# VectorE takes GpSimd's low halves and products in projections, decays, solves and output projection of a hybrid decoder

## The chip, the cores and the metric

The kernel runs on one core of a Trainium2 chip, in one launch. The metric is the device time of one execution in microseconds; each row of the trace gives times from the start of that execution. The engines are named as in the profile: PE is TensorE's matmul and PEld its weight load, DVE is VectorE, ACT is ScalarE, POOL is GpSimd, SP is SyncE, which issues the DMAs.

## The reference

The kernel computes a decoder trunk of two layers on one sequence of 1024 tokens of width 1024, with 16 learned tokens in front. Cut to what matters here:

```python
h = concatenate([meta, x])                                    # 1040 tokens
for layer in range(2):
    proj = rmsnorm(h) @ w_in[layer]                           # 1024 x 3336
    y_a = hgrn2_mixer(...)     # silu(q), gates, scores of chunks with decays
    y_b = gdn_mixer(...)       # conv of 4 taps, silu, l2norm, decays, a triangular solve per chunk
    y_c = s5_mixer(...)        # a complex scan, gelu, a gate
    h = h + concatenate([y_a, y_b, y_c]) @ w_out[layer]       # 1024 x 1024
    h = h + relu(rmsnorm(h) @ w1[layer])**2 @ w2[layer]       # 1024 x 4096 x 1024
return rmsnorm(h)[:, 16:]
```

All inputs and outputs are float32.

## The kernel before

The 1040 tokens are worked in two halves of 520 (`T`), with features on the 128 partitions and tokens along the free axis, so a tile is mostly 128x520. Within a half, the recurrent mixers go by five windows of 104 tokens (`W`).

**Weights in two parts.** TensorE multiplies in the type fp32r. Each operand is therefore split in a high half (`wh`, `xh`, `uh`: a cast) and a low half (`wl`, `xl`, `ul`: the operand minus its high half), and each product takes three matmuls: high by high, high by low, low by high (`columns`, L499). Weights come in granules of 128x512 (`granule_now`, L467): SP loads `wr` from DRAM, ACT casts `wh`, and POOL subtracts to make `wl` (L475 through `split`, L457). `wr`, `wh` and `wl` have three buffers each, so SP can load a granule only when the subtraction has read the one three before it, and ACT can cast one only when PE has used the one three before it. One column of the input projection is 128 output features and takes two granules, 48 matmuls. A half of a layer has 26 such columns (52 granules) and one narrow one of eight features (`cols_ab`); the output projection has 16 granules, the MLP 128.

**Stages.** `run` (L1424) issues for each layer and each half: `block` (the input projection, the mixers) and `out_mlp` (the output projection, the MLP). Nothing is ordered by hand: the compiler's scheduler places each instruction on its engine's queue, with the order of issue as the priority, and the weights are moved ahead by 1000 places (`granule`, L462). Each engine then works its queue in that order. In the trace the projections and mixers of layer 0 lie in 45 to 650 us (both halves), those of layer 1 in 1100 to 1400 us and in 1850 to 2200 us, with MLP stretches between and behind them.

**Within a block.** `normed_rows` (L506) makes the eight `xh`, `xl` pairs and carries four columns of history from one half to the next (`hist`, L518 to L523, copied by POOL). `in_conv` (L645) makes a column, takes the four taps on DVE out of PSUM (`s<-pd,cvw,s`), then `silu` (L576): exp, ln, exp on ACT, and a product, which POOL makes. `in_silu`, `in_gate` and `in_hgrn` use the same `silu` for their columns; in all it is called 80 times. Between the columns, `gdn_decay` (L825) makes each window's decay matrices: `nh<-nh,gtok` on DVE, abs and exp on ACT, on POOL a product with the triangular masks (`mh<-nh,tri`, 104x416) and one with beta (`mh<-mh,gsc`, 104x208), then on DVE the product with the scores in PSUM (`mh<-mxt,mh`). That is ten windows and pairs of heads in each block, forty in all. `gdn_solve` (L871) inverts the diagonal blocks of 26 by 26: twelve small steps on DVE, then two products of blocks in pieces of 80x507, of which POOL makes every second one (L902), and its result goes to DRAM as `XD` (L909). `s5_layer` (L356, first half of a layer only) makes the state-space matrices with many small DVE products. `hgrn` (L1137) and `gdn_state` (L913) are the recurrences; they use POOL as well.

Of the kernel before, what the change touches and what calls it, by code (L numbers as in the profile page):

```python
# [9 lines left out]
F32 = mybir.dt.float32  # L10
# [3 lines left out]
ALU = mybir.AluOpType  # L14
# [7 lines left out]
T = 520  # L22
W = 104
# [21 lines left out]
HIST = 4  # L45
# [49 lines left out]
class Kern:  # L95
# [91 lines left out]
    def setup(self):  # L187

        nc = self.nc
        self.take(T)  # L190
        self.K, self.XD, self.SC, self.grp = {}, None, None, "h"
        warm = self.n([128, 2, 128])
        nc.vector.memset(warm, 0.0)
        for _ in range(7):
            self.mm(self.mps()[:, :256], warm[:, 0], warm.rearrange("p a b -> p (a b)"))
        self.ident = self.load_const("ident", [128, 128])
        nc.scalar.preload_act_table_set("natural_log_exp_and_others")
# [269 lines left out]
    def granule_now(self, fill, keep):  # L467
        raw = self.tl(self.big, [128, 4, 128], "wr", N_W)
        fill(raw)
        if keep:  # L470
            lo, hi = [self.operand(tag)[:, :512].rearrange("p (k m) -> p k m", k=4) for tag in ("xl", "xh")]
        else:
            lo = self.tl(self.big, [128, 4, 128], "wl", N_W, F32R)
            hi = self.tl(self.big, [128, 4, 128], "wh", N_W, F32R)
        self.split(raw, hi, lo, self.nc.gpsimd)  # L475
        return hi, lo

    def weights(self, ap):
# [24 lines left out]
    def normed_rows(self, h, wcol, b):  # L503

        nc = self.nc
        xs = [], []  # L506
        acc = self.s()
        for k in range(KD):
            self.square(acc, h[k], k)
        self.squares, self.r = acc, None  # L510
        r = self.scale()
        if b == 0:
            self.hist = self.tl(self.big, [128, KD, HIST], "hist", 1)
        for k in range(KD):
            w = self.prm[:, wcol + k:wcol + k + 1]
            xn = self.tl(self.sp, [128, T + 8], "s", N_S)[:, :T + HIST]
            if b == 0:
                nc.gpsimd.memset(xn[:, :HIST], 0.0)  # L518
            else:
                nc.gpsimd.tensor_copy(xn[:, :HIST], self.hist[:, k])  # L520
            self.stt(xn[:, HIST:], h[k], w, r, ALU.mult, ALU.mult)
            if b == 0:
                nc.gpsimd.tensor_copy(self.hist[:, k], xn[:, T:])  # L523
            hi, lo = self.operand("xh"), self.operand("xl")
            nc.scalar.copy(hi, xn)
            self.tt(lo, xn, hi.bitcast(F32), ALU.subtract)
            xs[0].append(hi)
            xs[1].append(lo)
        return xs
# [45 lines left out]

    def silu(self, n, out):  # L576
        self.sigma(out, n)
        self.tt(out, out, n, ALU.mult, eng=self.nc.gpsimd)

    def cols(self, l, col, xs, runs=None):  # L580
        wts = self.ready.pop((l, col), None) or self.in_weights(l, col)
# [5 lines left out]
    def cols_ab(self, l, xs):  # L587


        nc = self.nc  # L590
        wi = self.ins["w_in"][l].rearrange("(g k p) m -> g p k m", k=4, p=128)
        ps = self.tl(self.pd, [128, 2, 512], "pd", 2)
        for g in range(2):
            raw = self.tl(self.big, [128, 4, 128], "wr", N_W)[:, :, :8]
            w = self.tl(self.big, [128, 4, 128], "wh", N_W, F32R)
            nc.sync.dma_start(raw, wi[g][:, :, C_GA:C_GA + 8])
            nc.scalar.copy(w[:, :, 0:32].rearrange("p k (r m) -> p k r m", r=4), raw.unsqueeze(2).to_broadcast([128, 4, 4, 8]))
            self.tt(w[:, :, 32:40], raw, w[:, :, 0:8].bitcast(F32), ALU.subtract, eng=nc.gpsimd)
            for k in range(4 * g, 4 * g + 4):
                for c in range(2):  # L600
                    cs = slice(HIST + c * HN, HIST + (c + 1) * HN)
                    self.mm(ps[0:40, c, :HN], w[:, k % 4, 0:40], xs[0][k][:, cs], start=(k == 0), stop=False)
                    self.mm(ps[0:40, c, :HN], w[:, k % 4, 0:40], xs[1][k][:, cs], start=False, stop=(k == KD - 1))
        return ps
# [220 lines left out]
    def gdn_decay(self, g, w, pair):  # L825
        nc, K = self.nc, self.K
        it = NW * pair + w
        h0 = 2 * pair
        hs, ws = slice(h0, h0 + 2), slice(w * W, (w + 1) * W)
        qk = self.m()[:, :4 * W].rearrange("p (a b) -> p a b", a=4)  # L830
        self.load_heads(qk, g, 2, h0, ws)
        bc = self.decay_rows(g, w, h0, W)
        yield
        E = self.n([W, 2, W])
        self.tt(E, bc, self.gtok[:, w, 0, hs].unsqueeze(2).to_broadcast([W, 2, W]), ALU.subtract)
        yield
        ps = self.mps("t")
        pg = ps[:W, :4 * W].rearrange("p (a b c) -> p a b c", a=2, b=2)
        for h in range(2):
            self.mm(pg[:, 0, h, :], qk[:, 2 + h, :], qk[:, 2 + h, :])  # L840
            self.mm(pg[:, 1, h, :], qk[:, 2 + h, :], qk[:, h, :])
        self.act(E, E, AF.Abs)
        self.act(E, E, AF.Exp, scale=-1.0)
        yield
        ln, b2 = self.gln[:, w, hs], self.gsc[:, w, 3, hs]
        sq = self.n([W, 2, W])
        self.tt(sq, pg[:, 0], self.ident[:W, :W].unsqueeze(1).to_broadcast([W, 2, W]), ALU.mult)
        nc.vector.tensor_reduce(ln, sq, mybir.AxisListType.X, ALU.add)
        self.act(ln, ln, AF.Ln, bias=EPS)
        self.act(b2, ln, AF.Exp, scale=-1.0)  # L850
        MA = self.m()[:W, :4 * W].rearrange("p (a b c) -> p a b c", a=2, b=2)
        self.tt(MA, E.unsqueeze(1).to_broadcast([W, 2, 2, W]), K["tri"].unsqueeze(2).to_broadcast([W, 2, 2, W]), ALU.mult, eng=nc.gpsimd)
        self.tt(b2, b2, self.gsc[:, w, 1, hs], ALU.mult)
        yield
        self.tt(MA[:, 0], MA[:, 0], b2.unsqueeze(2).to_broadcast([W, 2, W]), ALU.mult, eng=nc.gpsimd)
        self.tt(MA, pg, MA, ALU.mult)
        yield
        nc.sync.dma_start(self.item(self.MAd, it), MA)
        if w == NW - 1:
            for h in range(2):  # L860
                p0 = NBK * NW * (2 * h + pair)
                nc.sync.dma_start(self.diag[p0:p0 + NW * NBK], self.blocks(self.MAd, NW * pair, NW, h * W))
        yield
# [10 lines left out]
    def gdn_solve(self):  # L874

        nc = self.nc
# [3 lines left out]
        H = SB // 2  # L880
# [14 lines left out]
        low = lambda t: t[:, H:, 0:H]  # L895
        mid = self.n([80, H, H])
        for dst, a, bt in ((mid, low(Dg), Tm[:, 0:H, 0:H]), (low(Tm), Tm[:, H:, H:], mid)):
            for n, i0 in enumerate(range(0, H, 3)):
                k = min(3, H - i0)
                prod = tmp()[:, :k * H * H].rearrange("p (i c j) -> p i c j", i=k, c=H)  # L900
                self.tt(prod, bt.rearrange("p j c -> p c j").unsqueeze(1).to_broadcast([80, k, H, H]),
                        a[:, i0:i0 + k, :].unsqueeze(2).to_broadcast([80, k, H, H]), ALU.mult, eng=nc.gpsimd if n % 2 else None)  # L902
                nc.vector.tensor_reduce(dst[:, i0:i0 + k, :], prod, mybir.AxisListType.X, ALU.add)
        Tt = Dg
        nc.scalar.copy(Tt, Tm.rearrange("p a b -> p b a"))
# [373 lines left out]
    def out_mlp(self, l, b, h, last=False):  # L1279
        nc = self.nc  # L1280
# [7 lines left out]
        for m in range(KD):  # L1288
            ps = self.product(self.weights(self.ins["w_out"][l][:, 128 * m:128 * m + 128]), xs)
            self.tt(self.half(h[m]), self.half(h[m]), ps, ALU.add)  # L1290
        xs = self.normed(h, 16 + 8 * l)
        NG = D_FF // 512
        hid = {}
# [134 lines left out]
    def run(self):  # L1428
        self.setup()
        self.H, self.YS = {}, {}  # L1430
        nxt = {}

        def early():

            nxt[1] = self.htiles()
            yield from self.load_x(1, nxt[1])
            self.save_h(1, nxt[1])
        h = self.htiles()
        trace(self.load_x(0, h))
        self.ready = {(0, col): self.in_weights(0, col) for col in (C_SU, C_SU + 128)}  # L1440
        self.setup_norms()
        self.block(0, 0, h, early(), True)
        self.block(0, 1, nxt[1])
        for l in range(DEPTH):
            for b in range(NB):

                self.take(512 if l + 1 == DEPTH and b == 0 else T)
                h = self.get_h(b)
                steps = self.out_mlp(l, b, h, l + 1 == DEPTH and b + 1 == NB)
                if l + 1 < DEPTH:  # L1450
                    self.save_h(b, h)
                    self.block(l + 1, b, h)
                else:
                    self.finish(b, h, steps)
# [29 lines left out]
```

## Time and profile before

| what | value |
|---|---|
| median of 3 runs | 3055.49 us (3043.4 to 3062.02) |
| the profiled execution, its own time | 3057.18 us |
| its span, first to last instruction | 3055.4 us |
| PE busy | 2826.1 us, 92% |
| DVE busy | 1562.6 us, 51% |
| POOL busy | 1580.1 us, 52% |
| ACT busy | 1298.7 us, 43% |
| mean granted clock of TensorE | 0.964 |

The shares are means over stages with different limits: in the MLP stretches PE is busy all the time and the other engines have little to do; in the projections and mixers every engine has work and PE is idle now and then. PE's busy time is no measure of how fast it works, since the granted clock and the width of the matmuls differ. A number like "mean ns" of an instruction counts from its start to its end, with any time in which it was held after its start.

### The profile page before, as it was taken

Reading aid. Unit: us, or ns where it says so; the run is one execution under the profiler, and the core shown is the slowest. Engines: PE = TensorE matmul, PEld = TensorE weight load, DVE = VectorE, ACT = ScalarE, POOL = GpSimd, SP = SyncE. Lnnn points to the kernel's source line nnn. Section 1 sums busy time; section 2 is a strip of 40 time slices with the busy share of each in tenths; the row PEclk is TensorE's granted clock in tenths of the full one; section 3 lists DMA queues with packets and bytes.
Section 4 is the critical chain, followed back from the end, with each engine's and each line's share of the span. In section 5 each row is a group of like instructions: output and inputs, shape, how many; then the busy total and the mean of one; then the engine's idle time right before and its main releaser. Section 6 shows DMA issues by size and latency. Waiting matters only on the chain.

```text
span 3055.4 us, 60525 instructions
## 1 busy us (share of the span) xinstructions
PE 2826.1 (92%) x23513; PEld 2637.9 (86%) x23513; DVE 1562.6 (51%) x2905; ACT 1298.7 (43%) x2657; POOL 1580.1 (52%) x1425
## 2 busy tenths in 40 slices
PE   7776899979999989878999998988999999999998
PEld 6775889978999989878999998986777788999998
DVE  7588664685532245787453224686554222522224
ACT  4434455534433345444444334543544333433332
POOL 4555465664644445747354444676464444444442
PEclk8898899989999999999999999999999999999999
DMA  5755555744433345555443334565443333533332
GB/s 148 193 125 160 141 154 138 213 95 125 126 96 96 91 141 142 161 142 149 130 115 96 94 91 142 144 152 152 113 125 98 100 96 95 163 91 90 93 91 80
DMA packets 641610, 381.17 MB, mean 125 GB/s; under 512 B 166239, under 2 KB 599237, under 8 KB 641325
## 3 DMA queue, kind: packets, MB, share of 16 engines
q1 hardware_dynamic: 641325, 377.31, 45.2%
q8 instruction: 186, 3.05, 0.4%
q14 instruction: 99, 0.81, 0.1%
HBM read 308.52 MB, written 70.43 MB: 124 GB/s over the span
## 4 chain that ended last, share of the span: by engine, by line
PE 45%; DVE 5%; issue 1%; DMA 1%; POOL 1%; ACT 1%; SPq 0%; DVEq 0%; POOLq 0%; ACTq 0%
PE pd L125 39%; PE mxt L125 4%; PE mxh L125 1%; DVE mh L113 1%; DVE s L116 1%; POOL wl L113 0%; DVE s L113 0%; ACT s L110 0%; DMA wr<-in_w_in_dram 0%; DVE s L121 0%; DMA nh<-rowd 0%; DVE mt L113 0%; POOL mh L113 0%; DVE ul L113 0%; DVE s L642 0%
## 5 line engine op out<-in xcount | busy, mean ns | idle before, releaser
L113 POOL TENSOR_TENSOR wl<-wr,wh 128x512 fp32r<-128x512 f32 x776 | 1025.2, 1323 | 1079.5 <-ACT wh L459 1012.3
L125 PE MATMUL pd<-xh,wh 128*128 128x260 f32 (+4 forms) x3688 | 832.3, 299 | 59.2 <-DVE s L116 21.2
L125 PE MATMUL pd<-xl,wh 128*128 128x260 f32 (+3 forms) x3688 | 830.1, 298 | 17.8 <-DVE xl L113 10.4
L459 ACT CAST wh<-wr 128x512 fp32r<-128x512 f32 x776 | 477.5, 617 | 862.5 <-PE pd L125 774.5
L125 PE MATMUL pd<-xh,wl 128*128 128x260 f32 (+2 forms) x3624 | 814.1, 299 | 11.0 <-POOL wl L113 10.7
L125 PEld LDWEIGHTS pd<-xh,wh 128*128 128x128 f32 (+1 forms) x3688 | 593.1, 192 | 81.4 <-issue 28.6
L125 PEld LDWEIGHTS pd<-xl,wh 128*128 128x128 f32 (+1 forms) x3688 | 594.4, 192 | 34.4 <-DVE xl L113 12.3
L125 PEld LDWEIGHTS pd<-xh,wl 128*128 128x128 f32 x3624 | 586.3, 193 | 27.2 <-POOL wl L113 13.5
L125 PE MATMUL pd<-uh,wh 128*128 128x260 f32 (+1 forms) x2008 | 469.5, 302 | 6.2 <-DVE h L113 3.6
L125 PE MATMUL pd<-ul,wh 128*128 128x260 f32 (+1 forms) x2008 | 470.5, 302 | 0.0
L125 PE MATMUL pd<-uh,wl 128*128 128x260 f32 (+1 forms) x2008 | 468.5, 302 | 1.2 <-POOL wl L113 1.2
L113 DVE TENSOR_TENSOR h<-h,pd 128x520 f32<-128x520 f32 (+2 forms) x296 | 200.4, 678 | 398.1 <-PE pd L125 395.5
L110 ACT ACTIVATE s<-s 128x520 f32<-128x520 f32 (+3 forms) x431 | 272.9, 635 | 196.5 <-DVE s L121 144.8
L125 PEld LDWEIGHTS pd<-uh,wh 128*128 128x128 f32 x2008 | 321.2, 189 | 22.3 <-issue 5.9
L125 PEld LDWEIGHTS pd<-uh,wl 128*128 128x128 f32 x2008 | 321.2, 189 | 15.4 <-POOL wl L113 2.1
L125 PEld LDWEIGHTS pd<-ul,wh 128*128 128x128 f32 x2008 | 321.4, 189 | 12.8
L116 DVE SCALAR_TENSOR_TENSOR s<-pd,r 128x520 f32<-128x520 f32 (+2 forms) x121 | 83.6, 692 | 330.8 <-PE pd L125 330.5
L113 DVE TENSOR_TENSOR ul<-s,uh 128x520 fp32r<-128x520 f32 (+1 forms) x129 | 97.7, 758 | 143.4 <-ACT uh L459 143.2
L113 POOL TENSOR_TENSOR s<-s 128x520 f32<-128x520 f32 x80 | 109.6, 1370 | 78.7 <-ACT s L110 67.9
L116 DVE SCALAR_TENSOR_TENSOR s<-pd,cvw,s 128x520 f32<-128x520 f32 x144 | 108.6, 754 | 46.4 <-ACT s L110 41.6
L113 POOL TENSOR_TENSOR mh<-mh,qh 128x260 f32<-128x260 f32 (+5 forms) x128 | 102.8, 827 | 29.9 <-ACT mh L110 29.3
L113 DVE TENSOR_TENSOR s<-s 128x520 f32<-128x520 f32 (+3 forms) x119 | 106.0, 895 | 21.8 <-ACT s L110 20.5
(255 smaller groups left out, 3187.9 us busy)
## 6 DMA issues: line engine op xcount, KB each, us to landing
wr<-in_mlp_w_dram SPq DMA_DIRECT2D x512, 256.0 KB
wr<-in_w_in_dram SPq DMA_DIRECT2D x208, 256.0 KB
wr<-in_w_out_dram SPq DMA_DIRECT2D x64, 256.0 KB
qkvd<-s SPq DMA_DIRECT2D x48, 260.0 KB
win<-qkvd SPq DMA_DIRECT2D x40, 312.0 KB
hdr<-h SPq DMA_DIRECT2D x32, 260.0 KB
mh<-qkvd SPq DMA_DIRECT2D x40, 208.0 KB
hd<-s SPq DMA_DIRECT2D x32, 260.0 KB
```

The costliest lines, as they stand in the source:

```text
L110: return self.nc.scalar.activation(out, in_, func, **kw)
L113: return (eng or self.nc.vector).tensor_tensor(out, a, b, op)
L116: return self.nc.vector.scalar_tensor_tensor(out, a, s, b, op0, op1)
L125: return self.nc.tensor.matmul(out, lhsT, rhs, start=start, stop=stop, **kw)
L459: self.nc.scalar.copy(hi, src)
```

## The change

Eight kinds of work leave POOL; POOL keeps the low halves of the MLP's weights and the products of `hgrn`, `gdn_state` and `s5`.

```diff
@@ setup
+        self.low = None
@@ granule_now
-        self.split(raw, hi, lo, self.nc.gpsimd)
+        self.split(raw, hi, lo, self.low)
@@ normed_rows
-                nc.gpsimd.tensor_copy(xn[:, :HIST], self.hist[:, k])
+                nc.scalar.copy(xn[:, :HIST], self.hist[:, k])
...
-                nc.gpsimd.tensor_copy(self.hist[:, k], xn[:, T:])
+                nc.scalar.copy(self.hist[:, k], xn[:, T:])
@@ silu
-        self.tt(out, out, n, ALU.mult, eng=self.nc.gpsimd)
+        self.tt(out, out, n, ALU.mult)
@@ cols_ab
-            self.tt(w[:, :, 32:40], raw, w[:, :, 0:8].bitcast(F32), ALU.subtract, eng=nc.gpsimd)
+            self.tt(w[:, :, 32:40], raw, w[:, :, 0:8].bitcast(F32), ALU.subtract)
@@ gdn_decay
-        self.tt(MA, E.unsqueeze(1)..., K["tri"].unsqueeze(2)..., ALU.mult, eng=nc.gpsimd)
+        self.tt(MA, E.unsqueeze(1)..., K["tri"].unsqueeze(2)..., ALU.mult)
...
-        self.tt(MA[:, 0], MA[:, 0], b2.unsqueeze(2)..., ALU.mult, eng=nc.gpsimd)
+        self.tt(MA[:, 0], MA[:, 0], b2.unsqueeze(2)..., ALU.mult)
@@ gdn_solve
-                        a[:, i0:i0 + k, :].unsqueeze(2)..., ALU.mult, eng=nc.gpsimd if n % 2 else None)
+                        a[:, i0:i0 + k, :].unsqueeze(2)..., ALU.mult)
@@ out_mlp, behind the output projection
+        self.low = nc.gpsimd
@@ run, behind out_mlp
+                self.low = None
```

By count, 272 subtractions `wl` of 128x512, 8 of `xl<-wr,xh` (the last eight granules, which are issued behind the last `out_mlp`), 80 silu products of 128x520, 40 products of 104x416, 40 of 104x208, 16 of 80x507 and 8 small ones of `cols_ab` go from POOL to DVE; 32 copies of 128x4 go from POOL to ACT. POOL keeps 504 `wl`. The scheduler, given other engines, also places other instructions anew. Lines behind L191 stand one further down in the changed kernel.

On DVE, in layer 1's first half, between the columns of the convolution where the decays begin (`s<-pd,cvw,s` are the taps, `nh`, `gln` the decays), there stood before:

```order
L121 TENSOR_SCALAR s<-s 128x520
L116 SCALAR_TENSOR_TENSOR s<-pd,cvw,s 128x520 x3
L121 TENSOR_SCALAR s<-s 128x520
L113 TENSOR_TENSOR nh<-mxt,ident 104x208
L113 TENSOR_TENSOR nh<-nh,gtok 104x208
L848 TENSOR_REDUCE gln<-nh 104x2
L113 TENSOR_TENSOR nh<-mxt,ident 104x208
L848 TENSOR_REDUCE gln<-nh 104x2
L113 TENSOR_TENSOR nh<-nh,gtok 104x208
```

The same place now:

```order
L113 TENSOR_TENSOR wl<-wr,wh 128x512
L113 TENSOR_TENSOR mh<-nh,tri 104x416
L116 SCALAR_TENSOR_TENSOR s<-pd,cvw,s 128x520 x2
L113 TENSOR_TENSOR s<-s 128x520
L116 SCALAR_TENSOR_TENSOR s<-pd,cvw,s 128x520
L113 TENSOR_TENSOR wl<-wr,wh 128x512
L121 TENSOR_SCALAR s<-s 128x520
L113 TENSOR_TENSOR nh<-mxt,ident 104x208
L113 TENSOR_TENSOR nh<-nh,gtok 104x208
L849 TENSOR_REDUCE gln<-nh 104x2
L113 TENSOR_TENSOR nh<-mxt,ident 104x208
L113 TENSOR_TENSOR wl<-wr,wh 128x512
```

Two subtractions and one silu product stand in each column's row of taps, and the silu product of a column stands between the taps of the next.

On SP, in the same half, around the solve's results (`XD`), there stood before:

```order
L481 DMA wr<-in_w_in_dram 128x4x128 x2
L161 DMA hd<-s 128x520
L754 DMA qh<-hd 128x520
L909 DMA XD<-Tm 40x26x26 x2
L909 DMA XD<-diag 40x26x26 x2
L481 DMA wr<-in_w_in_dram 128x4x128 x2
```

and now:

```order
L482 DMA wr<-in_w_in_dram 128x4x128 x3
L910 DMA XD<-Tm 40x26x26 x2
L482 DMA wr<-in_w_in_dram 128x4x128
L910 DMA XD<-diag 40x26x26 x2
L482 DMA wr<-in_w_in_dram 128x4x128
```

One weight load stands between the two parts of `XD`, and four more weight loads of this half than before stand ahead of `XD`.

## Rows read from the trace of the kernel before

**Rows 1.** Busy time by stretch: three projection stages, and one of their densest parts.

```profile
core 0: us, PE busy (x) PEld busy (x) DVE busy (x) ACT busy (x) POOL busy (x), PEclk, DMA share, GB/s
45.00:650.00 605.00, 510.77 (x4587) 480.27 (x4585) 425.27 (x860) 299.85 (x674) 346.07 (x320) 0.93 0.58 153
1100.00:1400.00 300.00, 259.85 (x2044) 251.89 (x2044) 217.42 (x418) 142.94 (x286) 170.50 (x148) 0.94 0.58 153
1850.00:2200.00 350.00, 309.24 (x2494) 284.55 (x2494) 224.64 (x355) 170.47 (x345) 201.51 (x180) 0.94 0.54 142
...
1200.00:1300.00 100.00, 89.15 (x714) 86.95 (x713) 77.84 (x132) 49.77 (x112) 76.13 (x63) 0.97 0.61 166
```

**Rows 2.** What PE waited for in 45 to 650 us: total, times, longest.

```profile
PE mxh L125 <- DVE mh L113: 14.5, 5, 6.2
...
PE mxh L417 <- DVE nh L121: 10.8, 2, 9.6
PE pd L125 <- DVE s L116: 10.4, 5, 4.3
PE pd L125 <- POOL wl L113: 7.2, 6, 4.4
```

**Rows 3.** What PE waited for in 1100 to 1400 us.

```profile
PE pd L125 <- ACT wh L459: 7.8, 2, 7.2
```

**Rows 4.** POOL's groups of instructions, whole run: busy, mean ns, idle before.

```profile
L113 POOL TENSOR_TENSOR wl<-wr,wh 128x512 fp32r<-128x512 f32 x776 | 1025.2, 1323 | 1079.5 <-ACT wh L459 1012.3 <-PE pd L125 21.9 <-ACT nt L1003 4.7
L113 POOL TENSOR_TENSOR s<-s 128x520 f32<-128x520 f32 x80 | 109.6, 1370 | 78.7 <-ACT s L110 67.9 <-DVE Tm L894 10.3 <-PE pd L125 0.4
```

**Rows 5.** DVE's groups of instructions by shape, whole run.

```profile
L113 DVE TENSOR_TENSOR s<-s 128x520 f32<-128x520 f32 x73 | 69.2, 953 | 13.7 <-ACT s L110 12.8
...
L113 DVE TENSOR_TENSOR mh<-mxt,mh 104x416 f32<-104x416 f32 x40 | 23.2, 584 | 8.1 <-POOL mh L113 7.9
...
L113 DVE TENSOR_TENSOR xl<-s,xh 128x524 fp32r<-128x524 f32 x32 | 21.0, 692 | 1.1 <-ACT xh L525 0.9
```

**Rows 6.** DVE in order of time, 1219 to 1225 us: start, duration.

```profile
1220.63 0.75 DVE L116 SCALAR_TENSOR_TENSOR s<-pd,cvw,s 128x520 f32<-128x520 f32 x1
1221.30 2.10 DVE L113 TENSOR_TENSOR nh<-nh,gtok 104x208 f32<-104x208 f32 x1
1223.32 0.36 DVE L113 TENSOR_TENSOR nh<-mxt,ident 104x208 f32<-104x208 f32 x1
...
1223.67 0.42 DVE L121 TENSOR_SCALAR s<-s 128x520 f32<-128x520 f32 x1
```

**Rows 7.** POOL in order of time, the same stretch.

```profile
1220.61 1.32 POOL L113 TENSOR_TENSOR s<-s 128x520 f32<-128x520 f32 x1
1221.88 1.29 POOL L113 TENSOR_TENSOR wl<-wr,wh 128x512 fp32r<-128x512 f32 x1
```

**Rows 8.** DVE's groups of instructions by shape, 1200 to 1300 us.

```profile
L113 DVE TENSOR_TENSOR nh<-nh,gtok 104x208 f32<-104x208 f32 x9 | 7.7, 853 | 4.6 <-DMA nh<-rowd 4.6
L121 DVE TENSOR_SCALAR s<-s 128x520 f32<-128x520 f32 x8 | 6.8, 853 | 0.1
...
L113 DVE TENSOR_TENSOR mh<-Tm,diag 80x507 f32<-80x507 f32 x2 | 3.8, 1944 | 0.0
...
L113 DVE TENSOR_TENSOR gsc<-gsc,gln 104x20 f32<-104x20 f32 x1 | 3.3, 3272 | 0.0
...
L113 DVE TENSOR_TENSOR mh<-Tm,diag 80x8 f32<-80x8 f32 x1 | 1.1, 1133 | 0.0
...
L113 DVE TENSOR_TENSOR mh<-Tm,diag 80x50 f32<-80x50 f32 x1 | 0.2, 245 | 0.0
```

**Rows 9.** SP's DMA issues in order of time, 1290 to 1312 us.

```profile
1296.13 0.34 SPq L754 DMA_DIRECT2D qh<-hd  x1
1303.22 1.19 SPq L909 DMA_DIRECT2D XD<-Tm  x2
...
1308.52 2.44 SPq L481 DMA_DIRECT2D wr<-in_w_in_dram  x2
```

More of the change, by code (lines that the diff above doesn't have):

```diff
@@ L851, in gdn_decay @@
         MA = self.m()[:W, :4 * W].rearrange("p (a b c) -> p a b c", a=2, b=2)
-        self.tt(MA, E.unsqueeze(1).to_broadcast([W, 2, 2, W]), K["tri"].unsqueeze(2).to_broadcast([W, 2, 2, W]), ALU.mult, eng=nc.gpsimd)
+        self.tt(MA, E.unsqueeze(1).to_broadcast([W, 2, 2, W]), K["tri"].unsqueeze(2).to_broadcast([W, 2, 2, W]), ALU.mult)
         self.tt(b2, b2, self.gsc[:, w, 1, hs], ALU.mult)
         yield
-        self.tt(MA[:, 0], MA[:, 0], b2.unsqueeze(2).to_broadcast([W, 2, W]), ALU.mult, eng=nc.gpsimd)
+        self.tt(MA[:, 0], MA[:, 0], b2.unsqueeze(2).to_broadcast([W, 2, W]), ALU.mult)
         self.tt(MA, pg, MA, ALU.mult)
@@ L897, in gdn_solve @@
         for dst, a, bt in ((mid, low(Dg), Tm[:, 0:H, 0:H]), (low(Tm), Tm[:, H:, H:], mid)):
-            for n, i0 in enumerate(range(0, H, 3)):
+            for i0 in range(0, H, 3):
                 k = min(3, H - i0)
@@ L901, in gdn_solve @@
                 self.tt(prod, bt.rearrange("p j c -> p c j").unsqueeze(1).to_broadcast([80, k, H, H]),
-                        a[:, i0:i0 + k, :].unsqueeze(2).to_broadcast([80, k, H, H]), ALU.mult, eng=nc.gpsimd if n % 2 else None)
+                        a[:, i0:i0 + k, :].unsqueeze(2).to_broadcast([80, k, H, H]), ALU.mult)
                 nc.vector.tensor_reduce(dst[:, i0:i0 + k, :], prod, mybir.AxisListType.X, ALU.add)
```

## The prediction

> **What bounds the kernel now.** I read the stretches first, then what PE waited for in each, then the groups of POOL and DVE, and last the order of time at one crowded place. In the MLP stretches PE has no idle time, and the change leaves them as they are, so only the three projection stages count: 605, 300 and 350 us. PE is idle in them for 605 - 510.8 = 94.2, 300 - 259.9 = 40.1 and 350 - 309.2 = 40.8 us, 175 us together, and the granted clock is 0.93, 0.94 and 0.94, between the two levels of 1.2 and 2.4 GHz, which costs 605 x 0.07 + 300 x 0.06 + 350 x 0.06 = 81 us more [rows 1]. So about 256 us can be had or doubled; the rest is matmul time. In these stages DVE is busy 425 + 217 + 225 = 867 of 1255 us, or 69%, and POOL 718 us [rows 1]. PE waits mostly for DVE: for `hgrn`'s tiles 14.5 us, for the matrices of `s5_layer` 10.8, for the taps 10.4; for POOL's low halves 7.2 [rows 2]. In layer 1 the largest wait is one of 7.2 us for a cast of weights [rows 3].
>
> What makes DVE late is seen in order of time. At 1221.30 a product of 104x208 with both inputs in SBUF takes 2.10 us; the next product, of the same shape but with one input in PSUM, takes 0.36 [rows 6]. Through the first POOL runs a silu product (1220.61 to 1221.93) and then a `wl` (1221.88 to 1223.17), and the DVE product ends 0.2 us after the second [rows 7]: it was held until POOL was done. A simple operation on one tile is held as well: `s<-s` has a mean of 853 ns here, where one takes 0.42 us [rows 6, 8]. The tap next to it, which reads PSUM, took its 0.75 us with POOL at work. By the Trainium skill (SBUF — State Buffer, "Who interferes with whom"), a VectorE instruction with two SBUF inputs and a GpSimd one that reads SBUF exclude each other, and the later one waits for the whole of the other; the 2.10 us agree, and show that it can be passed over twice.
>
> **The change part by part.** *Work added to DVE.* The nearest price of a `wl` is `xl<-s,xh`, 128x524 with both inputs in SBUF: 692 ns [rows 5]. At the crowded place the next instruction starts 0.67 us after one that lasts 0.75, so ends overlap and each one costs DVE about 0.09 us less than it lasts [rows 6]; I take 0.60. A high bound is the mean of the silu-like products that DVE makes now, 953 ns with POOL in the way [rows 5]. So: 280 subtractions and 80 silu products x 0.60 = 216 us; 40 products of 104x416 at 584 - 90 = 0.49 [rows 5], 20 us; 40 of 104x208 at 0.36 - 0.09 = 0.27 [rows 6], 11 us; 16 of 80x507, not seen free, between 0.69 for as many elements in a dense tile [rows 5] and 1.94 as held now [rows 8], taken at 1.2 since their operands are read with strides, 19 us. In all 266 us, bounds 230 and 370. Some 250 of it falls in the three stages (the other subtractions stand in layer 1's last output projection, the tail and the first microseconds).
>
> *Time that DVE gets back.* In 1200 to 1300 us all of POOL's 76.1 us is work that leaves it [rows 1]. There nine `nh<-nh,gtok` lose 9 x (853 - 360) = 4.4 us, eight `s<-s` 8 x (853 - 420) = 3.5, one of 20 elements most of 3.3, two of the solve 2 x (1.94 - 1.2) = 1.5, and an 80x8 product took 1133 ns where one of 80x50 took 245 [rows 6, 8]: 13.5 us, and a number of single ones as the last; I estimate 20. DVE now stands at 77.8. Added there is about 76.1 x 0.60/1.35 = 34 (the ratio of the new price to POOL's means of 1323 and 1370 ns [rows 4]). So 77.8 + 34 - 20 = 92 of 100 us. Over the three stages, with the relief scaled by POOL's busy time, 718/76.1 x 20 = 189, of which I count 60%, as POOL's own `hgrn` and state products go on holding DVE: 867 + 250 - 113 = 1004, 80% in place of 69%. DVE becomes fuller, not emptier; what improves is that a result comes when its turn comes, not up to 2 us later, and that POOL's 1.3 us per product become 0.69.
>
> *What this is worth to PE, by wait.* (1) POOL's `wl`: it is ready 1.32 - 0.69 = 0.6 us sooner, and no longer behind a silu product; 5 of 7.2 us [rows 2]. (2) The 7.2 us for a cast: SP stood on `XD` from 1296.5 until the solve ended at 1303.2, and no weight was loaded until 1308.5 [rows 9]. The solve loses its held products, and the order puts a weight load between the parts of `XD` and more loads ahead; 7 us over the two halves of layer 1. (3) `s5_layer`'s matrices, 10.8 us: DVE comes late to a place that PE's order has fixed; 8 us. (4) `hgrn`, 14.5 us: half of POOL's work in its way goes, the rest is `hgrn`'s own; 7 us. (5) Against it: the taps, 10.4 us in the first stage, and the like in the others wait in a fuller queue, with two `wl` and a product per column; 10 us more. A `wl` that waits for ACT's cast holds the taps, decays and scans behind it; the cover is the three buffers, which put a cast two granules ahead of its use. (6) The remaining 134 us of idle time have the same mix of causes; I take 10 us of it. Together -5 -7 -8 -7 +10 -10 = -27 us, and, as the clock has fallen with idle time so far, 27 x 81/175 = 12 or 13 us more: -40.
>
> *At nothing.* The 32 copies to ACT are of 128x4, on an engine busy half of each stage [rows 1]; even at 0.36 us each, the smallest price here [rows 6], they make 12 us that only count beside the first column of a half. The eight subtractions of the tail come between DVE's last products and would cost 8 x 0.6 = 5 us at most, about what these lose now to POOL's.
>
> The profiled execution is 3057.2 us, 1.7 above the median, so no correction is made: 3057 - 40 = 3017 us.
>
> **The rivals.** *A, slower: DVE becomes the bound.* Were nothing given back, the dense 100 us would need 77.8 + 34 = 112 us of DVE. Each block has one such stretch (decays and solve), and without overlap of ends it is 77.8 + 39 = 117: 4 x 12 to 17 = 48 to 68 us, less about 10 for (1): 3105 us. It decides from the point where DVE's share in the stretch passes 95%, as PE's columns then wait for their taps and SP's loads for `wl`. For it: 92 is near, and DVE idled there only for data. Against it: the held instructions are plain to see.
>
> *B, no change.* What DVE gets back is what it has to do more: 250 against at most 189. PE's waits only change names; gains (1) and (2) pay for (5): 3050 us. The Trainium skill (Perfetto Trace Analysis, "Optimizing Scalar/DVE Operations") speaks for this: since the two engines share a read port, work moved between them may not help. For it: 94 of 256 us are idle time of the first stage, in which loads of tokens and the chain of a first column also wait. Against it: POOL needs about twice DVE's time for the same work [rows 4, 5], so the sum of both falls.
>
> *C, a large gain.* If lateness is what the order suffers from, all waits that the named rows stand for shrink by half: 175/2 + 81/2 = 128 us, less 10 for (5): 2940 us. For it: the order was made once, and each held instruction shifts all behind it. Against it: the fuller DVE.
>
> *D, that it doesn't do what it says*: the order shows every `wl` of projections on DVE and none on POOL, so I give it nothing.
>
> **How the numbers follow.** Likeliest, 3017 us, with a range of its own of 2985 to 3040: 0.48. A 0.18, B 0.22, C 0.12. About 1% (30 us) is what a measurement of this kernel can tell from no change. Faster by over 1% (under 3025): 0.38 of the 0.48, C's 0.12, and 0.04 of B make 0.54. Slower by over 1% (over 3086): 0.14 of A and 0.01 of B, 0.15. Within: 0.31. The range of 2955 to 3090 leaves out half of C and most of A, together about 0.19.
>
> **What would show it.** Right: POOL's busy time falls by about 600 us and DVE's rises by some 100 to 150; `nh<-nh,gtok` and `s<-s` come near 370 and 420 ns in the decays; PE waits hardly at all for `wl`; PE's idle time in the projection stages is near 145 us, the granted clock there 0.94 or 0.95; the MLP stretches are the same. Wrong: DVE over 95% in the decays, PE waiting for DVE's `wl` or taps for more than 50 us in all (A), or idle time as before (B). If DVE's `wl` have a mean over 0.8 us, POOL still holds them and the price of the first term was too low.

## The result and the profile after

The changed kernel takes 3003.66 us (median of 4 runs, 3001.06 to 3009.43) beside 3053.48 us of the kernel before on the same chip: ratio 0.9838, 95% interval 0.9808 to 0.9868. The forecast was 3017 us. The profiled execution is 3006.09 us with a span of 3004.3, against 3057.18 and 3055.4.

First the busy time of the engines, from the page:

```profile
PE 2820.8 (94%) x23513; PEld 2639.4 (88%) x23513; DVE 1624.5 (54%) x3369; ACT 1305.5 (43%) x2689; POOL 979.8 (33%) x929
```

POOL has lost 600 us (1580.1 before) and DVE has gained only 62 (1562.6 before). The span less PE's busy time, which is PE's idle time, was 3055.4 - 2826.1 = 229.3 us and is 3004.3 - 2820.8 = 183.5: 46 of the 51 us came from idle time, 5 from faster matmuls.

The stretches, which answer to [rows 1] (moved, since the work comes earlier; the last is as dense as the last of those):

```profile
core 0: us, PE busy (x) PEld busy (x) DVE busy (x) ACT busy (x) POOL busy (x), PEclk, DMA share, GB/s
45.00:640.00 595.00, 526.72 (x4700) 497.42 (x4698) 459.17 (x1072) 308.93 (x690) 98.24 (x109) 0.92 0.59 158
1080.00:1380.00 300.00, 268.27 (x2134) 263.16 (x2132) 232.77 (x526) 148.83 (x297) 24.85 (x27) 0.95 0.58 156
1815.00:2160.00 345.00, 311.23 (x2539) 287.54 (x2539) 250.94 (x478) 177.91 (x365) 62.89 (x60) 0.96 0.55 148
1185.00:1285.00 100.00, 92.21 (x758) 91.07 (x757) 86.93 (x191) 52.11 (x116) 0.00 (x0) 0.98 0.60 159
```

PE's idle time is 68.3, 31.7 and 33.8 us, 134 together, where it was 175. The last line is the one to read slowly: in 100 us DVE does 191 instructions where it did 132, and is busy for 87 us where it was for 78. It did 45% more instructions in 12% more busy time. The two forms that [rows 8] shows at 853 ns, in this stretch:

```profile
L113 DVE TENSOR_TENSOR nh<-nh,gtok 104x208 f32<-104x208 f32 x9 | 3.4, 373 | 3.8 <-DMA nh<-rowd 3.8
...
L121 DVE TENSOR_SCALAR s<-s 128x520 f32<-128x520 f32 x6 | 2.6, 429 | 0.0
```

DVE's groups by shape over the whole run (busy, mean ns | idle before) answer to [rows 5]:

```profile
L113 DVE TENSOR_TENSOR wl<-wr,wh 128x512 fp32r<-128x512 f32 x272 | 189.6, 697 | 59.7 <-ACT wh L460 54.8 <-ACT mt L110 2.2 <-DMA h<-hdr 1.0
...
L113 DVE TENSOR_TENSOR s<-s 128x520 f32<-128x520 f32 x153 | 110.9, 728 | 40.2 <-ACT s L110 38.7 <-DMA gated<-s 0.4
...
L121 DVE TENSOR_SCALAR s<-s 128x520 f32<-128x520 f32 x52 | 23.0, 443 | 0.2
...
L113 DVE TENSOR_TENSOR nh<-nh,gtok 104x208 f32<-104x208 f32 x40 | 14.9, 372 | 19.2 <-DMA nh<-rowd 13.9 <-ACT gtok L798 5.3
```

The silu-like products have a mean of 728 ns where it was 953, though 80 of these 153 are the ones that came from POOL. In order of time, a row of instructions like that of [rows 6] now reads (start, duration):

```profile
1200.70 0.38 DVE L113 TENSOR_TENSOR nh<-mxt,ident 104x208 f32<-104x208 f32 x1
1200.98 0.38 DVE L113 TENSOR_TENSOR nh<-nh,gtok 104x208 f32<-104x208 f32 x1
1201.26 0.70 DVE L113 TENSOR_TENSOR s<-s 128x520 f32<-128x520 f32 x1
1201.87 0.77 DVE L116 SCALAR_TENSOR_TENSOR s<-pd,cvw,s 128x520 f32<-128x520 f32 x1
```

The product with two SBUF inputs, 2.10 us in [rows 6], takes as long as its neighbour with one input in PSUM. What PE waited for in the first stage, answering to [rows 2]:

```profile
PE mxh L434 <- DVE mh L113: 10.6, 2, 8.6
PE mxh L125 <- DVE mh L113: 6.2, 2, 4.1
...
PE pd L125 <- DVE s L116: 3.7, 2, 2.4
PE pd L125 <- ACT wh L460: 3.2, 1, 3.2
...
PE pd L125 <- DVE wl L113: 1.0, 1, 1.0
```

and in layer 1's first block, answering to [rows 3]:

```profile
PE pd L125 <- DVE s L116: 8.5, 7, 2.7
PE pd L125 <- DVE mh L113: 6.2, 1, 6.2
...
PE pd L125 <- ACT wh L460: 0.3, 1, 0.3
```

### The profile page after: what moved, and what is told of

Same layout as the page of the kernel before. It is cut to its first block, busy times and chain, and to the rows that moved or that the text cites. A ratio compares the mean times of both kernels' runs of the same rounds, so it can differ in the third digit from the quotient of the medians.

```text
span 3004.3 us, 60331 instructions
## 1 busy us (share of the span) xinstructions
PE 2820.8 (94%) x23513; PEld 2639.4 (88%) x23513; DVE 1624.5 (54%) x3369; ACT 1305.5 (43%) x2689; POOL 979.8 (33%) x929
## 4 chain that ended last, share of the span: by engine, by line
PE 48%; DVE 3%; DMA 2%; issue 0%; ACT 0%; SPq 0%; POOL 0%; DVEq 0%; ACTq 0%; POOLq 0%
PE pd L125 42%; PE mxt L125 4%; PE mxh L125 1%; DVE mh L113 1%; DVE s L116 1%; DMA XD<-diag 0%; DVE wl L113 0%; DVE s L113 0%; PE mxt L1374 0%; DMA nh<-rowd 0%; DVE ul L113 0%; DVE xl L113 0%; DMA D<-D 0%; DMA wr<-in_w_out_dram 0%; DMA wr<-in_mlp_w_dram 0%
## 5 line engine op out<-in xcount | busy, mean ns | idle before, releaser
L113 POOL TENSOR_TENSOR wl<-wr,wh 128x512 fp32r<-128x512 f32 x504 | 659.7, 1310 | 929.6 <-ACT wh L460 773.7
L125 PE MATMUL pd<-xh,wh 128*128 128x260 f32 (+3 forms) x3688 | 832.8, 300 | 49.0 <-DVE s L116 20.9
L125 PE MATMUL pd<-xl,wh 128*128 128x260 f32 (+4 forms) x3688 | 829.6, 298 | 6.9 <-DVE xl L113 6.4
L125 PE MATMUL pd<-xh,wl 128*128 128x260 f32 (+2 forms) x3624 | 810.3, 298 | 5.8 <-DVE wl L113 3.8
L125 PEld LDWEIGHTS pd<-xh,wh 128*128 128x128 f32 (+1 forms) x3688 | 593.7, 192 | 70.7 <-issue 21.2
L125 PEld LDWEIGHTS pd<-xl,wh 128*128 128x128 f32 (+1 forms) x3688 | 594.9, 192 | 22.8 <-DVE xl L113 7.7
L125 PEld LDWEIGHTS pd<-xh,wl 128*128 128x128 f32 x3624 | 585.8, 193 | 20.0 <-DVE wl L113 4.5
L125 PE MATMUL pd<-uh,wh 128*128 128x260 f32 (+1 forms) x2008 | 470.0, 303 | 8.3 <-ACT uh L460 5.6
L125 PE MATMUL pd<-uh,wl 128*128 128x260 f32 (+1 forms) x2008 | 471.1, 302 | 1.2 <-DVE wl L113 1.2
L125 PE MATMUL pd<-ul,wh 128*128 128x260 f32 (+1 forms) x2008 | 471.7, 302 | 0.0
L125 PEld LDWEIGHTS pd<-uh,wh 128*128 128x128 f32 x2008 | 322.7, 190 | 23.3 <-ACT uh L460 5.8
L125 PEld LDWEIGHTS pd<-uh,wl 128*128 128x128 f32 x2008 | 322.7, 189 | 14.6 <-DVE wl L113 1.4
L125 PEld LDWEIGHTS pd<-ul,wh 128*128 128x128 f32 x2008 | 322.7, 189 | 13.4
L113 DVE TENSOR_TENSOR wl<-wr,wh 128x512 fp32r<-128x512 f32 x272 | 189.6, 697 | 59.7 <-ACT wh L460 54.8
L113 DVE TENSOR_TENSOR s<-s 128x520 f32<-128x520 f32 (+3 forms) x199 | 141.0, 711 | 48.3 <-ACT s L110 46.6
L113 POOL TENSOR_TENSOR nt<-nt 128x208 f32<-128x208 f32 x80 | 52.9, 661 | 206.6 <-ACT nt L110 96.6
```

What stands on the lines that cost most here:

```text
L113: return (eng or self.nc.vector).tensor_tensor(out, a, b, op)
L125: return self.nc.tensor.matmul(out, lhsT, rhs, start=start, stop=stop, **kw)
```

## The experiments

Two theories stood against each other. *Holding* (H in the first expectations): a GpSimd instruction that reads SBUF stops DVE's instructions beside it, and the gain is the end of that. *Queue* (L and A there): what counts is where the work stands and how much of it; POOL was slow, its results came late, and a fuller DVE costs time. Ratios are to the kernel before, beside which each run stood.

**Unused products on POOL.** DVE keeps all work that the change gave it; POOL makes two products per weight tile that nobody reads.

```diff
         self.split(raw, hi, lo, self.low)
+        if self.low is None and not keep:
+            idle = self.tl(self.sp, [128, 4, 52], "idle", 1)
+            a, b = [hi[:, :, 52 * i:52 * i + 52].bitcast(F32) for i in range(2)]
+            for _ in range(2):
+                self.tt(idle, a, b, ALU.mult, eng=self.nc.gpsimd)
```

> Leaves nothing out; adds work that nobody uses: for each granule of the projections POOL multiplies two quarters of wh (128x208, twice, about 0.66 us each, so about what one wl took), while VectorE makes the low halves as in the changed kernel. Theory H (the gain came from VectorE no longer being held while POOL reads SBUF): held instructions are back, on top of VectorE's added work, so nh<-nh,gtok has a mean over 550 ns again and the time is 3040 to 3090 us. Theory L (the gain came from each low half and each silu product being ready 0.65 us sooner): nothing in the chain waits for POOL's idle products, so 3000 to 3012 us.

Measured: 3063.42 us, 1.0059 (1.004 to 1.0078). The whole gain is gone, and some more, as *holding* said. But it isn't clean: `nh<-nh,gtok` rose only to 422 ns, not over 550 as expected, and ACT, which casts the high halves, now waited for the new products to let go of a buffer (26.2 us of its idle time):

```profile
L460 ACT CAST wh<-wr 128x512 fp32r<-128x512 f32 x776 | 478.8, 618 | 900.0 <-PE pd L125 803.8 <-issue 34.2 <-POOL idle L113 26.2
```

**The low halves alone**, and **all but the low halves**: the first is the kernel before with `self.low`, the second the changed kernel with this line as it was.

```diff
-        self.split(raw, hi, lo, self.low)
+        self.split(raw, hi, lo, self.nc.gpsimd)
```

> Only the low halves of the projections' and output projections' weights (and of the last eight granules) go to VectorE; silu products, decays, solve, history stay on POOL. H: the gain goes with POOL's busy time that leaves it, some 370 of 600 us, so about 30 of 50 us: 3015 to 3030. L: the wait for POOL's wl was 12 us in all, so 3038 to 3045. Theory A (VectorE's fuller queue costs): the 170 us more on VectorE without the relief of the decays, 3055 or more.

> All of the change but the low halves, which stay on POOL. H: 230 of POOL's 600 us go, about 20 of 50 us: 3028 to 3040. L: the columns' chains end sooner by 0.65 us each, half of the gain: 3025 to 3030, and nh<-nh,gtok stays over 550 ns. A: little is added to VectorE, no loss.

Measured: 3005.19 us, 0.9869 (0.9849 to 0.9889), and 3034.39 us, 0.9969 (0.9956 to 0.9982). The low halves are worth 1.3%, the rest 0.3%; together 1.6%, as the whole change. *Holding*, shared out by POOL's busy time, said 30 and 20 us; they are 39 and 10. So the silu products and the decays, at which the holding was first seen in [rows 6, 7], are the small part of it, and POOL's busy time doesn't say what a piece is worth.

**The changed kernel again, MLP's low halves on DVE too, `hgrn`'s products on DVE too, and both.** The first of the edits also stands in the earlier set of runs:

```diff
@@ out_mlp, behind the output projection
-        self.low = nc.gpsimd
@@ hgrn, six places
-        self.tt(o, o, fac, ALU.mult, eng=nc.gpsimd)
+        self.tt(o, o, fac, ALU.mult)
```

> The changed kernel with the MLP's 504 low halves on VectorE as well, so POOL makes only the products of the recurrences. H: the recurrences that lie beside the MLP (650 to 900, 1400 to 1650, 2100 to 2350 us) are held less; PE idles there for only some 15 us, so 2990 to 3002. L: as now, 3000 to 3008. A: VectorE's queue now holds a wl in front of every step of the recurrences, slower than 3010.

> The changed kernel itself, on the same chip as the next three, so that they can be set against it: 0.981 to 0.987 of the kernel before.

> The changed kernel with the MLP's low halves on VectorE as well (232 more tiles at about 0.7 us). Holding (a GpSimd operation slows VectorE's beside it, and PE waits for those): the MLP stretches carry hgrn steps too, whose VectorE operations are then free, so 10 to 25 us below the changed kernel beside it. Queue (what counts is only how much VectorE has to do): VectorE's share rises by 9 points and PE waits more for it, so the same as the changed kernel or above it by up to 20 us.

> The changed kernel with hgrn's own GpSimd products (f, P, the level factors of 128x240 to 128x260, gt) on VectorE; the MLP's low halves stay on GpSimd. Holding: these products are what still holds VectorE in hgrn, PE's waits for mh made by VectorE fall from about 40 us to under 25, 8 to 20 us below the changed kernel. Queue: the products only join VectorE's queue ahead of the subtractions of the next level, which PE waits for next, within 6 us of the changed kernel or above it.

> Both of the last two. Holding: nearly nothing of GpSimd's is left beside hgrn, 15 to 40 us below the changed kernel. Queue: VectorE's share reaches about 92 per cent of the span with nothing taken off it, at least 20 us above the changed kernel.

Measured: MLP's alone, in the earlier set, 2986.99 us, 0.9813 (0.9795 to 0.9832), below every range written for it; the kernel before took 3044.53 us there, 9 less than beside the changed kernel. Then, on one chip:

| kernel | median, us | ratio to before | 95% interval |
|---|---|---|---|
| changed kernel again | 2994.08 | 0.9814 | 0.9797 to 0.9831 |
| MLP's low halves too | 2986.43 | 0.9792 | 0.9778 to 0.9805 |
| `hgrn`'s products too | 2990.94 | 0.9806 | 0.9792 to 0.9821 |
| both | 2967.65 | 0.9727 | 0.9713 to 0.974 |

Each alone is worth less than *holding* said (8 and 3 us, within the intervals); for `hgrn`'s products the 3 us are what *queue* said. Both together are worth 26, and beat both kernels. That a fuller DVE costs time falls with the last line: DVE is busy 297 us more than in the changed kernel, and the time falls. Two numbers written there were slips: DVE's busy time, 1922.1 us, is 65% of the span, not 92%, and the MLP's low halves are 504 tiles, not 232. In the changed kernel, run again, and in the last, PE's idle time stands in these stretches (the MLP's first two, then the projections):

```profile
640.00:1070.00 430.00, 419.93 (x4050) 402.80 (x4050) 174.19 (x352) 168.60 (x352) 217.22 (x208) 0.99 0.40 108
1370.00:1800.00 430.00, 423.06 (x4064) 405.00 (x4065) 177.33 (x346) 168.15 (x356) 214.33 (x207) 0.98 0.40 111
...
45.00:635.00 590.00, 521.05 (x4707) 491.84 (x4705) 460.61 (x1074) 308.87 (x690) 100.21 (x109) 0.93 0.58 159
1070.00:1370.00 300.00, 271.02 (x2164) 266.05 (x2163) 232.42 (x527) 150.35 (x300) 26.29 (x29) 0.96 0.57 157
1800.00:2150.00 350.00, 317.48 (x2594) 294.09 (x2593) 253.28 (x480) 179.22 (x367) 66.47 (x63) 0.96 0.54 149
```

```profile
640.00:1070.00 430.00, 423.74 (x4084) 407.21 (x4085) 246.29 (x500) 167.73 (x351) 46.70 (x61) 0.99 0.40 109
1370.00:1800.00 430.00, 428.16 (x4168) 412.07 (x4167) 248.60 (x501) 171.69 (x361) 45.08 (x60) 1.00 0.41 115
...
45.00:635.00 590.00, 530.76 (x4749) 502.72 (x4748) 466.60 (x1119) 311.79 (x697) 53.68 (x63) 0.92 0.58 159
1070.00:1370.00 300.00, 276.06 (x2206) 270.83 (x2205) 240.37 (x550) 155.06 (x307) 4.45 (x12) 0.96 0.58 158
1800.00:2150.00 350.00, 321.30 (x2538) 291.50 (x2537) 264.56 (x531) 180.00 (x374) 25.46 (x28) 0.96 0.55 149
```

It falls in all five: by 3.8 and 5.1 us in the MLP's, by 9.7, 5.0 and 3.8 in the projections. PE's wait for what DVE makes in `hgrn` (`mxh`, L125, for `mh`) shows the same in the run with both:

```profile
PE mxh L125 <- DVE mh L113: 2.9, 2, 2.2
```

It was 18.8 us in the changed kernel beside it, 9.2 with the MLP's moved and 5.6 with `hgrn`'s. Why two edits that shorten this wait alone hardly show in the time stays open.

**Fills, copies, and everything on DVE.** The first two are the changed kernel with other work for POOL in the place of the two unused products (the diff shows each, cut to that work). The third is the kernel with both edits of the last table, with `gdn_state`'s and `s5`'s products and the low halves of small operands (`pl`) on DVE as well.

```diff
+            for _ in range(7):
+                self.nc.gpsimd.memset(idle, 0.0)
...
+            for i in (0, 1, 0, 1):
+                self.nc.gpsimd.tensor_copy(idle, hi[:, :, 52 * i:52 * i + 52].bitcast(F32))
```

> The changed kernel, where GpSimd fills a small tile of its own (128x208) seven times for each weight tile whose low half VectorE makes: about as long busy as with the two unused products per tile, but reading nothing. If the holding comes from what GpSimd's two-operand instructions read: 0.980 to 0.988, as the changed kernel, and nh<-nh,gtok stays near 370 ns. If any busy GpSimd holds VectorE: 0.995 to 1.01, as with the unused products.

> As the last, with four unused copies of 128x208 out of the high half (one operand read, none computed) in place of the seven fills. If two read operands are what it takes: 0.980 to 0.988. If one is enough: 0.993 to 1.01.

> Every two-operand operation of GpSimd on VectorE (the last ones: nt, mt, pl, and the one above them); it has only fills and small copies left. Holding: VectorE's operations nowhere slowed; these products sit in stretches where VectorE is half free, so 0.968 to 0.974, up to 10 us below the kernel with MLP's and hgrn's moved. Queue: in the first layer's projections VectorE has no room for them, 0.975 to 0.985.

Measured: fills 2994.88 us, 0.9844 (0.9828 to 0.986), as the changed kernel; copies 3091.34, 1.0167 (1.0152 to 1.0183), beyond both ranges written for it; everything on DVE 2962.99, 0.9739 (0.9723 to 0.9754), no better than both edits above. The copies' loss can't be put down to holding alone, as PE's waits show:

```profile
PE pd L125 <- DVE wl L113: 54.0, 47, 5.0
...
PE pd L125 <- ACT wh L460: 13.3, 16, 2.1
```

DVE's `wl` was late because ACT's cast was, for which a buffer was missing: 46.6 us of ACT's idle time ended with POOL's copies. `nh<-nh,gtok` has 423 ns there and `s<-s` of two tiles 768, so the copies hold DVE too, but how much of the 3% that is stays open.

**Products of POOL's own.** The clean form of the first experiment: nothing of the weights is read, and no buffer kept.

```diff
+        self.own = self.big.tile([128, 208], F32, name="own")
+        nc.gpsimd.memset(self.own, 0.0)
...
+            for _ in range(2):
+                self.tt(self.own, self.own, self.own, ALU.mult, eng=self.nc.gpsimd)
```

> The changed kernel, where GpSimd multiplies a small tile of its own (128x208) with itself twice for each weight tile whose low half VectorE makes: as many products of that size as in the run with unused products, but none reads the weights' high half, so no buffer of the weights is kept by them and nothing waits for them. If that run's loss was the holding of VectorE by GpSimd's operand reads: 0.995 to 1.008, and VectorE's forms longer than in the changed kernel (nh<-nh,gtok above 400 ns, s<-s 128x520 above 760). If it came from the buffers that the unused products kept: 0.980 to 0.988, with VectorE's forms as in the changed kernel.

Measured: 3045.66 us, 1.0008 (0.9998 to 1.0018): the gain is gone. Over the run `nh<-nh,gtok` has 408 ns and `s<-s` of two tiles 779, just above the bounds written for *holding*. Since these products wait for nothing, nearly all stand in the first stage, and most of the fills do as well, so the two runs can be set against each other there. With the fills, the stretch of 45 to 640 us and DVE's groups in it:

```profile
45.00:640.00 595.00, 527.57 (x4714) 497.81 (x4713) 468.97 (x1072) 310.19 (x690) 463.49 (x1442) 0.92 0.58 158
```

```profile
L113 DVE TENSOR_TENSOR wl<-wr,wh 128x512 fp32r<-128x512 f32 x116 | 81.6, 704 | 23.9 <-ACT wh L460 23.1 <-PE pd L125 0.4
...
L121 DVE TENSOR_SCALAR s<-s 128x520 f32<-128x520 f32 x24 | 12.4, 515 | 0.1
L113 DVE TENSOR_TENSOR nh<-nh,gtok 104x208 f32<-104x208 f32 x20 | 7.4, 369 | 10.0 <-DMA nh<-rowd 6.9 <-ACT gtok L802 2.9
```

and with the products:

```profile
45.00:640.00 595.00, 487.88 (x4263) 454.59 (x4264) 486.84 (x981) 285.74 (x643) 447.13 (x606) 0.89 0.54 146
1080.00:1380.00 300.00, 273.41 (x2174) 268.68 (x2173) 201.75 (x460) 145.93 (x287) 36.13 (x36) 0.96 0.55 149
```

```profile
L113 DVE TENSOR_TENSOR wl<-wr,wh 128x512 fp32r<-128x512 f32 x108 | 86.4, 800 | 22.7 <-ACT wh L462 21.4 <-PE pd L125 1.0
...
L121 DVE TENSOR_SCALAR s<-s 128x520 f32<-128x520 f32 x24 | 14.6, 610 | 0.1
L113 DVE TENSOR_TENSOR nh<-nh,gtok 104x208 f32<-104x208 f32 x16 | 7.5, 468 | 5.7 <-DMA nh<-rowd 3.2 <-ACT gtok L803 2.5
```

POOL is busy equally long, 463 and 447 us, and PE is idle for 67 us beside fills, as in the changed kernel, and for 107 beside products; DVE does 981 instructions in more busy time than 1072. In layer 1, where no such product stands, PE's idle time is 26.6 us. So products that read SBUF do it, and fills that keep POOL as busy don't. That POOL's other results come late can be only a small part of the 40 us: PE's waits that end with an instruction of POOL are 6.7 us in all beside fills and 4.1 beside products, ACT's 11 and 20. That the time lands on the kernel before is chance: the products crowd into the first stage, where PE's idle time is above the 94 us of the kernel before, and layer 1 keeps its gain. One wait grew most: `s5_layer`'s matrices.

```profile
PE mxh L436 <- DVE mh L113: 25.7, 2, 22.4
```

## Why the prediction was right, and where its sum was off

The direction stands. So does its cause, as far as the runs go: beside fills the gain stays, beside products that read SBUF it goes. How much of the 50 us the holding is, and how much that DVE makes a product in half of POOL's time, they don't separate. The two signs came as written, 373 ns for `nh<-nh,gtok` and 429 for `s<-s` of one tile in the dense stretch; POOL fell by 600 us as said. The time came out 50 us below the kernel before in place of 40. By its steps:

- *Work added and given back.* DVE's busy time rose by 62 us, not by 100 to 150. The `wl` cost 697 ns against the 692 of their nearest row, so if the added work was as counted, DVE got back 867 + 250 - 943 = 174 us in the stages, where 113 were counted. In the dense stretch it got back 77.8 + 34 - 86.9 = 25 in place of 20. The relief was the mis-sized term, most of all by "of which I count 60%": the products that POOL kept leave it busy for only 98, 25 and 63 us in these stages. DVE's share is 943 of 1240 us, 76% in place of 80%, and 87 of 100 in the dense stretch in place of 92. The low bound of 230 us for the added work doesn't follow from its terms, of which 216 + 20 + 11 are 247 already.
- *(1) POOL's `wl`*: 7.2 us to 1.0 in the first stage, for -5 predicted. *(2) The cast*: 7.8 to 0.3 in layer 1's first block and 4.4 to nothing in its second, 12 us for -7. SP's loads now go on between the parts of `XD`, as written. *(3) `s5_layer`*: the wait for `nh` (10.8 us) is gone, for -8, but the one for the products behind it rose from 5.6 to 10.6 in the first stage, so the two fell by 6 us together. Two of these waits of the kernel before, in layer 1's second block and in the first stage, in the order named:

```profile
PE pd L125 <- ACT wh L459: 4.4, 2, 3.9
...
PE mxh L433 <- DVE mh L113: 5.6, 2, 3.1
```

- *(4) `hgrn`*: 14.5 to 6.2 in the first stage, for -7. But over the whole run this wait only went from 20.2 to 22.7 us: what the first stage gained, later stretches lost. Over the run it shrinks only in the kernels in which the MLP's low halves or `hgrn`'s own products have left POOL too.
- *(5) The taps, +10*, failed: 3.7 in the first stage for 10.4, 8.5 and 8.6 in the two others for 5.5 and 5.2, nothing in all. DVE did more instructions, but its busy time in the stages rose by 76 us only.
- *Sum and clock.* Idle time in the stages fell by 41 us, not 27. Over the three stages the waits of (1) to (5) fell by 7, 11, 12, 5 and 0 us, 35 in all, and 6 are left for all others, where (6) took 10. That (5) and (6) cancel in the sum, and neither came so, is luck. The clock gave less than said: 0.92, 0.95 and 0.96 cost 595 x 0.08 + 300 x 0.05 + 345 x 0.04 = 76 us where it was 81, so 5 us and not 12. In the first stage it even fell a hundredth while idle time fell, so scaling the clock's cost with the idle time doesn't hold.
- *The MLP stretches* were not without idle time, as the section on the time before and the prediction's first paragraph had it: before, the first two had 12.8 and 9.5 us.

```profile
650.00:1100.00 450.00, 437.23 (x4197) 419.78 (x4198) 188.94 (x357) 174.80 (x363) 229.97 (x217) 0.99 0.40 106
1400.00:1850.00 450.00, 440.48 (x4201) 422.78 (x4201) 183.44 (x341) 174.57 (x362) 225.76 (x211) 0.98 0.39 109
```

  The change itself does little there; in the changed kernel run again, 430 - 419.9 = 10.1 and 430 - 423.1 = 6.9 us are left, which the run with both edits takes to 6.3 and 1.8.
- *The rivals.* A needed 95% of DVE in the dense stretch and got 87. B said that what DVE gets back is what it has to do more; in the stages 174 us came back for 250. By the Trainium skill (Perfetto Trace Analysis, "Optimizing Scalar/DVE Operations") moving work between the two engines might not help as they share a port. Here it gave 1.6 to 1.9%, and a further 0.9% with the next two pieces: POOL's `wl` takes 1.32 us [rows 4], DVE's 0.70, and each one off POOL also frees DVE. C's 2940 us were not reached, not even with everything on DVE.

## What to carry to other kernels

When VectorE's durations of one shape spread between a shortest and several times that, look at what GpSimd reads at that moment before counting busy shares: moving GpSimd's two-operand work to VectorE can pay though VectorE is the fuller engine. Price the move by the shortest duration of the form, and credit VectorE with most of what its other instructions lost beside GpSimd (174 us here, where 189 were estimated). Fills could stay on GpSimd here; one piece that is left there can hide what the next one would give, so try the pieces together too.

## What was not expected of the hardware

- The holding goes both ways. GpSimd's private product takes 525 ns at the least and 536 in the median, but one took 7.97 us, while VectorE worked off some sixteen instructions without a gap:

```profile
L113 POOL TENSOR_TENSOR own<-own x544: 525/536/7965, 3.3 to 561.2; 128x208 f32<-128x208 f32 x182
```

- Fills leave products with two SBUF inputs alone (`nh<-nh,gtok` 369 ns beside them, 371 without), but not the scaling of one tile: `s<-s` has 515 ns beside fills in the first stage and 442 in the changed kernel. The Trainium skill (SBUF — State Buffer, "Who interferes with whom") separates the two: two-input instructions contend with GpSimd's reads alone, those in a mode with two ports with any use of the shared pair. Both means agree with it, if the scaling runs in such a mode, which no run here shows.
- An unused reader can cost by the buffer that it keeps, as far as the waits tell: with four unused copies per tile, PE waited 54 us for DVE's `wl`, though making one took hardly longer (722 ns for 697).
